# A hybrid attention and state-space layer: second group of weight blocks taken three pairs at a time instead of two

## The chip, the cores and the metric

One Trainium2 chip, of which the kernel uses one core. The metric is device time in microseconds, median of the runs.

## The reference

One layer of a streaming encoder on x of 1024 tokens by 2048 features, float32. One input projection gives everything; half of the width goes through sparse attention, half through a Mamba-2 scan; one output projection and a LayerNorm end it. Cut to what matters here:

```
u = jnp.einsum('bsd,de->bse', h, w_in[layer])            # 2048 x 6752
q, k, v, z_attn, q_idx, k_idx, w_idx, z_ssd, xbc, dt_raw = _split_cols(u, IN_WIDTHS)
o_attn = _dsa_attention(q, k, v, q_idx, k_idx, w_idx) * jax.nn.silu(z_attn)   # indexer, top 256 keys, softmax
o_ssd = _ssd_mixer(xbc, z_ssd, dt_raw, ...)              # conv, scan in chunks, gated norm
mixed = jnp.concatenate([o_attn, o_ssd], axis=-1)
sub = jnp.einsum('bse,ed->bsd', mixed, w_out[layer])
h = _layer_norm(DEEPNORM_ALPHA * h + sub, ln_g[layer], ln_b[layer])
```

## The kernel before, in words

**Products.** Weights and activations are split into a high and a low part (`wh`, `wl`; `xh`, `xl`), and a float32 product is three matmuls: high by high, high by low, low by high. A block of weights is 128 output columns by 1024 features, so one product of a block with 512 tokens is 8 x 3 = 24 matmuls of 512 columns into one PSUM bank. The high part is a copy on ACT, the low part a subtraction on DVE, seldom on POOL (`w_split`).

**Fewer products.** Two output tiles, two halves of the features and two halves of the tokens make a 2 x 2 x 2 problem that the kernel solves with seven products instead of eight (Strassen, in Winograd's form). So output tiles go in pairs. `PLAN` has two groups of pairs: the first (index 0) of eight, the second (index 1) of fourteen, numbered 0 to 13 here: 0 to 5 are the scan's x, B and C (`xbc`), 6 to 13 gates (`zs` with `z`).

**Stages.** A group runs in four stages (`ph` 0 to 3). In stages 0, 1 and 2 every pair has two products (`f` 0 and 1, here the pair's *first* and *second* product). They take two sets of x: stage 0 the two halves of x, stage 1 the sums M2 and M3, stage 2 the sums S1 and S4. In stage 3 a pair has one product. The second product of a pair goes on in the PSUM bank of its first: the first opens it, and its partial result has to be read out before the second goes on. In stage 0 ACT reads it (`t_save`, an ACTIVATE `u<-pj`, then a DMA to DRAM); in stage 1 DVE adds a saved sum to it (`t_u`), in stage 2 too (`t_comb`), both a TENSOR_TENSOR `u<-pj,u`. The second product waits for that (`p.after` in `emit_t`). Within a stage the pairs are taken in `couples`: the first products of all pairs of a couple, then their second ones.

**Weights.** A product of stage 0 loads one block; a first product of stage 1 loads three, of which two sums are made on DVE or POOL (`t_wacc`): one is for it, the other stays in its `wr` buffer for the pair's second product. In stage 2 a first product loads two and keeps one. There are six `wr` buffers for raw blocks, three `wh`, three `wl` (line 592). PSUM has four banks `pj` for the products, three `a` and one `o` for the rest; sums of attention and scan that find no `o` may take a `pj` while three or more are free (`avail`, `new`).

**The order of the work.** `Layer.run` walks the list of products that `units` made, 24 matmuls in four parts. Ahead of each part `Flow.pump` lets tasks run (generators that yield what they need next): copies, top-k, scan, attention, weight sums. A task may go ahead when the engine it needs is no further past PE by the kernel's own clock than a fixed slack (`SLACK` in `Flow.ready`, doubled for priority 0). So the instruction order of every engine is fixed when the program is built, with a model of times that also decides between DVE and POOL (`pick`), and a change in the list of products moves all later work. On the chip each engine runs its own list in order and waits on semaphores. While the second group starts, the top-k search over four blocks of keys runs on ACT, in counts (`u<-s,sm`, `u<-u,sm`: a Sign with a sum) whose thresholds DVE sets between them, and the scans of the first tokens start.

All instructions are issued through one helper, so each carries line 312; the names of the tiles tell them apart.

Of the kernel before, what the change touches and what calls it, by code (L numbers as in the profile page):

```python
# [582 lines left out]
class Layer:  # L583
# [20 lines left out]
    def units(self):  # L604

        pieces, work = [], []
        self.hooks = {}
        self.sets = []
        self.mate = {}

        def put(p, listed=True):
            if listed:
                work.append((len(pieces), None))
            pieces.append(p)
            return len(pieces) - 1

        def plain(h, tile, u, n):
            kind, j = tile
            t = ORDER.index(tile)
            p = Piece("T", h, t, u, load=(("w", t, u),), n=n + u, open=u == 0, close=u == 1, key=(h, t),  # L620
                      s0=256 if (kind == "qi" and h == 0) else 0)
            if u == 1:
                p.done = lambda ps: self.fl.add(getattr(self, "t_" + kind)(h, j, ps), 0, f"{kind}{j}h{h}", self.fl.t + 100)
            put(p)

        for pairs in PLAN:
            if isinstance(pairs, tuple):
                h, tiles, end = pairs
                n = len(self.sets)
                self.sets += [("x", h, 0), ("x", h, 1)]  # L630
                for part in [tiles[:3]] + [[t] for t in tiles[3:-end]] + [tiles[-end:]]:
                    for u in range(2):
                        for tile in part:
                            plain(h, tile, u, n)
                continue
            gi = GROUPS.index(pairs)
            if self.sets[-2:] != [("x", 0, 0), ("x", 0, 1)]:
                self.sets += [("x", 0, 0), ("x", 0, 1)]
            base = len(self.sets) - 2
            self.sets += [("f", "M2"), ("f", "M3"), ("f", "S1"), ("f", "S4"), ("x", 1, 1)]  # L640
            couples = [list(range(c, min(c + 2, len(pairs)))) for c in range(0, len(pairs), 2)]
            if len(couples[-1]) == 1:
                couples[-2:] = [couples[-2] + couples[-1]]
            for ph in range(4):
                if (gi, ph) in ((0, 2), (1, 0)):
                    self.hooks.setdefault(len(pieces), []).append(lambda on=gi == 0 and ph == 2: setattr(self.fl, "resting", on))
                for couple in [int(k) if k.isdigit() else k for k in OPENING] if (gi, ph) == (0, 0) else couples:
                    if isinstance(couple, str):
                        tile = ("misc", 0) if couple == "m" else QI["abcdefgh".index(couple)]
                        for u in range(2):  # L650
                            plain(0, tile, u, base)
                        continue
                    couple = couples[couple] if isinstance(couple, int) else couple
                    for f in range(1 + (ph < 3)):
                        for c in couple:
                            i = put(self.product(gi, c, pairs[c], ph, f, base + 2 * ph + f))
                            if f:
                                self.mate[gi, c, ph] = i
                            if ph and (ph, f) != (1, 1):
                                self.hooks.setdefault(max(i - 1, 0), []).append(lambda gi=gi, c=c, ph=ph, f=f: self.pre_ld(gi, c, ph, f))  # L660
        end = {}
        for i, p in enumerate(pieces):
            end[p.n] = i
        for i in end.values():
            pieces[i].last = True
        freed = sorted(end, key=end.get)
        for n in range(2, len(self.sets)):
            at = end[freed[n - 2]] - 2
            self.hooks.setdefault(at, []).append(lambda n=n: self.request(n))
        self.n_t = len(pieces)  # L670
        self.hooks.setdefault(self.n_t - 6, []).append(lambda: self.forms(0))
        self.hooks.setdefault(12, []).append(self.form_tasks)
        for half in range(2):
            self.hooks.setdefault(12, []).append(lambda half=half: self.fl.add(self.t_wsum(half), 5, "wsum"))
        for n in range(7):
            for d in range(2):
                for j in range(4):
                    if n < 6 or 4 * d + j < 8 - SKEW:
                        work.append((len(pieces), (0, 1, 2, 3)))
                    name = PRODUCTS[n][1]  # L680
                    pieces.append(Piece("O", n, d, j, load=(("o", name, d, j),)))
        for sts in ((0,), (1,), (2,), (3,)):
            work += [(len(pieces) - SKEW + j, sts) for j in range(SKEW)]
        return pieces, work
# [1672 lines left out]
```

## Time and profile before

| | us |
|---|---|
| median of 3 runs | 1664.8 (1663.27 to 1667.5) |
| profiled execution | 1667.98, its span 1666.1 |
| PE busy | 1620.1 (97% of the span) |
| DVE busy | 1321.7 (79%) |
| ACT busy | 1002.0 (60%) |
| POOL busy | 197.3 (12%) |
| mean granted TensorE clock | 0.992 |

The first group ends and the second begins at about 573 us; its stages 0, 1, 2 and 3 run to about 769, 1008, 1219 and 1313 us, and the output projection follows. A timeline row has start and length in us, engine, line, operation, out<-in, shape, count, and in brackets how long the engine stood idle before it and what ended that. Matmuls overlap in the pipeline, so their rate is read from start to start and not from their length. A row of the windows has the stretch, then the busy time of PE, PEld (weight loads), DVE, ACT and POOL with their instructions in brackets, the granted clock, the share of DMA and GB/s.

### The profile page before, as it was taken

How to read it: one execution, taken by the hardware profiler on the slowest of the kernel's cores; microseconds unless marked ns; L12 is line 12 of the kernel's file. 1: busy time of each engine (PE TensorE's matmuls, PEld its weight loads, DVE VectorE, ACT ScalarE, POOL GpSimd, SP SyncE). 2: the span in 40 equal slices, each digit the busy share in tenths (PEclk: the TensorE clock that was granted, in tenths of full speed). 3: DMA queues.
4: the chain of work that ended last, by engine and by line, in shares of the span. 5: the costliest groups of instructions: out<-in, count | busy, mean ns of one | idle time of the engine just before them, and what ended most of it. 6: DMA issues, size and time to landing. Idle time of an engine off the chain costs nothing. (4 is left out here: it accounts for less than half of the span.)

```text
span 1666.1 us, 23979 instructions
## 1 busy us (share of the span) xinstructions
PE 1620.1 (97%) x7996; PEld 1340.9 (80%) x7996; DVE 1321.7 (79%) x2429; ACT 1002.0 (60%) x1770; POOL 197.3 (12%) x215
## 2 busy tenths in 40 slices
PE   9999999999998989999999999999999999999997
PEld 7787777888787768888888888888877888888885
DVE  5889998997778866788676669875787687659998
ACT  4555666779787788776344456776866555532330
POOL 0100010000000000122212202222010000100110
PEclk9999999999999999999999999999999999999999
DMA  8177574789768856687786584656988889668664
GB/s 309 52 280 258 189 262 168 268 303 334 290 230 324 294 196 234 235 304 277 260 288 218 180 286 161 210 171 210 334 284 307 316 300 325 215 232 274 220 202 152
DMA packets 192387, 414.48 MB, mean 249 GB/s; under 512 B 19720, under 2 KB 55688, under 8 KB 192264
## 3 DMA queue, kind: packets, MB, share of 16 engines
q1 hardware_dynamic: 191832, 412.56, 71.7%
q8 instruction: 63, 1.03, 0.2%
q14 instruction: 60, 0.49, 0.1%
q10 hardware_dynamic: 432, 0.39, 0.1%
HBM read 308.94 MB, written 103.94 MB: 248 GB/s over the span
## 5 line engine op out<-in xcount | busy, mean ns | idle before, releaser
L312 PE MATMUL pj<-xh,wh 128*128 128x512 f32 (+1 forms) x1496 | 585.7, 392 | 14.5 <-ACT u L312 6.0
L312 PE MATMUL pj<-xh,wl 128*128 128x512 f32 (+1 forms) x1496 | 573.6, 383 | 5.1 <-DVE wl L312 5.1
L312 PE MATMUL pj<-xl,wh 128*128 128x512 f32 (+1 forms) x1496 | 573.0, 383 | 0.0
L312 DVE TENSOR_TENSOR wl<-wr,wh 128x1024 fp32r<-128x1024 f32 (+2 forms) x236 | 282.4, 1201 | 172.4 <-ACT wh L312 170.4
L312 PEld LDWEIGHTS pj<-xh,wh 128*128 128x128 f32 x1496 | 283.8, 190 | 68.6 <-issue 7.5
L312 PEld LDWEIGHTS pj<-xh,wl 128*128 128x128 f32 x1496 | 283.5, 190 | 63.1 <-DVE wl L312 7.3
L312 PEld LDWEIGHTS pj<-xl,wh 128*128 128x128 f32 x1496 | 284.0, 190 | 49.1
L312 ACT ACTIVATE wh<-wr 128x1024 fp32r<-128x1024 f32 (+2 forms) x242 | 248.1, 1031 | 120.0 <-PE pj L312 82.8
L312 PE MATMUL a<-u,u 128*128 128x512 f32 (+3 forms) x736 | 172.8, 354 | 7.6 <-DVE s L312 4.4
L312 PEld LDWEIGHTS a<-u,u 128*128 128x128 f32 x736 | 120.7, 189 | 42.5 <-DVE s L312 18.6
L312 ACT ACTIVATE u<-a 128x512 fp32r<-128x512 f32 (+4 forms) x115 | 53.2, 479 | 153.3 <-DVE u L312 58.0
L312 ACT ACTIVATE u<-s,sm 128x640 bf16<-128x640 int16 (+7 forms) x132 | 129.7, 983 | 22.1 <-DVE sm L312 20.0
L312 DVE TENSOR_TENSOR u<-u,u 128x512 f32<-128x512 f32 (+6 forms) x204 | 128.6, 645 | 5.7 <-DMA u<-wo 1.3
L312 PE MATMUL pj<-wh,xh 128*128 128x512 f32 x310 | 125.2, 404 | 0.5 <-DVE u L312 0.5
L312 PE MATMUL pj<-wh,xl 128*128 128x512 f32 x310 | 121.0, 390 | 0.0
L312 PE MATMUL pj<-wl,xh 128*128 128x512 f32 x310 | 121.0, 390 | 0.0
L312 ACT ACTIVATE a<-a 128x512 f32<-128x512 f32 (+3 forms) x160 | 77.1, 505 | 68.3 <-PE a L312 65.5
L312 ACT ACTIVATE u<-u 128x512 f32<-128x512 f32 (+4 forms) x146 | 80.1, 558 | 52.4 <-DVE u L312 43.9
L312 DVE TENSOR_TENSOR u<-pj,u 128x512 f32<-128x512 f32 (+2 forms) x112 | 74.7, 668 | 45.7 <-PE pj L312 42.2
L312 DVE TENSOR_TENSOR wr<-wr,wr 128x1024 f32<-128x1024 f32 (+1 forms) x81 | 99.8, 1233 | 0.8 <-DMA wr<-wt 0.4
L312 POOL TENSOR_SCALAR s<-s,sm 128x640 f32<-128x640 f32 (+7 forms) x64 | 63.8, 1011 | 124.0 <-DVE sm L312 97.4
L312 DVE SCALAR_TENSOR_TENSOR u<-cv,cw,u 128x512 f32<-128x512 f32 x96 | 73.0, 766 | 6.7 <-ACT u L312 3.5
(259 smaller groups left out, 2200.3 us busy)
## 6 DMA issues: line engine op xcount, KB each, us to landing
wr<-wt SPq DMA_DIRECT2D x187, 512.0 KB
u<-u SPq DMA_DIRECT2D x110, 256.0 KB
wr<-t SPq DMA_DIRECT2D x44, 512.0 KB
u<-wo SPq DMA_DIRECT2D x64, 256.0 KB
ts<-u SPq DMA_DIRECT2D x64, 256.0 KB
wr<-ts SPq DMA_DIRECT2D x32, 512.0 KB
s<-xt SPq DMA_DIRECT2D x24, 512.0 KB
t<-wr SPq DMA_DIRECT2D x22, 512.0 KB
```

Source lines behind the costliest of these rows:

```text
L312: f(*args, **kw)
```

## The change

In `units`, where the pairs of a group are cut into couples, the length goes from 2 to 2 + `gi`, the index of the group. The first group keeps its couples of two. The second has five runs in place of seven couples: pairs 0-2, 3-5, 6-8, 9-11 and 12-13. The rule for a last couple of one pair, below it, does not apply in either.

```
-            couples = [list(range(c, min(c + 2, len(pairs)))) for c in range(0, len(pairs), 2)]
+            couples = [list(range(c, min(c + 2 + gi, len(pairs)))) for c in range(0, len(pairs), 2 + gi)]
```

So in stages 0 to 2 the list reads: first products of pairs 0, 1, 2, second products of 0, 1, 2, first products of 3, 4, 5, and so on; before it was first 0, 1, second 0, 1, first 2, 3. Stage 3 is the same list as before. What the kernel's scheduler makes of it shows on every engine from there on. ACT in stage 0, before: the rows from the copy of pair 2's first product (`pj_1047`) to that of pair 3 (`pj_1053`); `s4_953` is a tile of the scan, `u_538` and `u_684` outputs of the top-k counts, `wh_...` high parts of weights.

```order
L312 ACTIVATE u_1049_6044<-pj_1047_6006 128x512
L312 ACTIVATE u_538_2976,sm_537_2975<-s4_109_745,sm_537_2975 128x896
L312 ACTIVATE u_538_2976,sm_537_2975<-s4_110_746,sm_537_2975 128x1024
L312 ACTIVATE wh_1051_6053<-wr_1009_5787 128x1024
L312 ACTIVATE u_684_3785,sm_683_3784<-u_440_2425,sm_683_3784 128x384
L312 ACTIVATE u_684_3785,sm_683_3784<-u_441_2426,sm_683_3784 128x512
L312 ACT_TABLE_LOAD
L312 ACTIVATE u_958_5501<-s4_953_5496 64x512 x2
L312 ACTIVATE s4_953_5496<-s4_953_5496,ac0_241 128x128 x8
L312 ACTIVATE u_1055_6107<-pj_1053_6057 128x512
L312 ACTIVATE wh_1056_6110<-wr_1024_5856 128x1024
```

And after, from the weights of pair 8's first product (`wh_1100`) to the copy of pair 6's (`pj_1103`):

```order
L312 ACTIVATE wh_1100_6413<-wr_1071_6180 128x1024
L312 ACT_TABLE_LOAD
L312 ACTIVATE u_958_5501<-s4_953_5496 64x512 x2
L312 ACTIVATE s4_953_5496<-s4_953_5496,ac0_241 128x128 x8
L312 ACT_TABLE_LOAD
L312 ACTIVATE u_1099_6401<-u_1099_6401 128x512
L312 ACTIVATE wh_1109_6474<-wr_1075_6213 128x1024
L312 ACTIVATE u_1112_6485<-pj_1103_6419 128x512
```

The scan's instructions on `s4_953` stood ahead of the copy of pair 3 and stand ahead of that of pair 6 now.

DVE in stage 1, before: up to the low part of the weights (`wl_1604`) for pair 8's first product; `pj_1582` is the bank of pair 7.

```order
L312 TENSOR_TENSOR sm_1583_8844<-sm_1583_8844 128x2
L312 TENSOR_SCALAR sm_1583_8844<-sm_1583_8844 128x2
L312 TENSOR_TENSOR u_1591_8896<-a_1589_8892,u_1590_8895 128x256
L312 TENSOR_TENSOR u_1599_8929<-pj_1582_8834,u_1552_8714 128x512
L312 TENSOR_TENSOR u_1595_8912<-a_1593_8906,u_1594_8911 128x512
L312 TENSOR_TENSOR u_1598_8922<-a_1596_8916,u_1597_8921 128x512
L312 RECIPROCAL sm_1583_8844<-sm_1583_8844 128x2
L312 TENSOR_TENSOR wl_1604_8945<-wr_1519_8541,wh_1603_8944 128x1024
```

And after, where `wl_1561` is that low part and `pj_1537` the bank of pair 7:

```order
L312 SCALAR_TENSOR_TENSOR u_1487_8398<-u_1487_8398,dn_222,o_1541_8691 128x256 x2
L312 TENSOR_TENSOR u_1518_8543<-u_1518_8543,u_1558_8780 128x512
L312 TENSOR_TENSOR u_1517_8541<-u_1517_8541,u_1518_8543 128x512
L312 TENSOR_TENSOR u_1559_8790<-pj_1537_8675,u_1535_8648 128x512
L312 TENSOR_TENSOR wl_1561_8795<-wr_1523_8581,wh_1560_8794 128x1024
L312 TENSOR_TENSOR wl_1563_8799<-wr_1468_8282,wh_1562_8798 128x1024
L312 TENSOR_TENSOR wl_1565_8803<-wr_1507_8454,wh_1564_8802 128x1024
```

In both the low part follows the sum that reads pair 7's first product; the products that stand between the two on PE are two before and none after.

## Prediction

> **What bounds the kernel now.** I read the page first, then the chain of waits for the tensor engine alone, cut to the second group (573 to 1313 us), then the timeline of PE and ACT where the longest waits end, then the windows for the clock.
>
> ```profile
> span 1666.1 us, 23979 instructions
> PE 1620.1 (97%) x7996; PEld 1340.9 (80%) x7996; DVE 1321.7 (79%) x2429; ACT 1002.0 (60%) x1770; POOL 197.3 (12%) x215
> ```
>
> PE is busy for 97% of the span, so at most 46 us of the span are idle PE, and an edit that adds and drops no work can win only from that idle and from matmuls that run slower than they could. In the second group, PE's waits, longest first (us in total, times, longest):
>
> ```profile
> PE pj L312 <- ACT u L312: 6.0, 2, 4.3
> PE a L312 <- DVE u L312: 2.1, 2, 1.5
> PE pj L312 <- ACT wh L312: 1.6, 1, 1.6
> ```
>
> The first row is 6.0 us in two waits alone; no row left out here is over 1.1. ACT's `u<-pj` is the copy of a pair's first product out of its PSUM bank (`t_save`, stage 0), and the waiting matmul is the first of the same pair's second product, which goes on in that bank. PE around the two:
>
> ```profile
> 583.38 0.39 PE L312 MATMUL pj<-xl,wh 128*128 128x512 f32 x1
> 583.60 0.39 PE L312 MATMUL pj<-xh,wl 128*128 128x512 f32 x1
> 585.73 0.50 PE L312 MATMUL pj<-xh,wh 128*128 128x512 f32 x1 [1.74 <-ACT u L312]
> ...
> 613.66 0.59 PE L312 MATMUL a<-u,u 128*128 128x256 f32 x2
> 618.56 0.80 PE L312 MATMUL pj<-xh,wh 128*128 128x512 f32 x1 [4.31 <-ACT u L312]
> 619.15 0.63 PE L312 MATMUL pj<-xl,wh 128*128 128x512 f32 x1
> ...
> 624.27 0.54 PE L312 MATMUL pj<-xl,wh 128*128 128x512 f32 x1
> 624.65 0.39 PE L312 MATMUL pj<-xh,wl 128*128 128x512 f32 x1
> 624.88 0.40 PE L312 MATMUL pj<-xh,wh 128*128 128x512 f32 x1
> ```
>
> In front of 585.73 the matmuls start 0.22 us apart (583.38, 583.60), so the next was due at 583.83: 1.90 us lost. The two 256-column matmuls at 613.66 were over in the queue by 613.90 (0.12 each, by half the 512-column step), and the next starts at 618.56: 4.66 us lost. It isn't over there: from 619.15 to 624.65 13 matmuls start in 5.50 us, 0.42 apart, where the full rate takes 2.95, and the one before took 0.59, so another 2.9 us go. The windows (span, busy PE, PEld, DVE, ACT, POOL, PEclk, DMA share, GB/s) say why:
>
> ```profile
> 573.00:590.00 17.00, 15.27 (x68) 12.32 (x67) 14.95 (x22) 14.72 (x28) 0.49 (x1) 1.00 0.66 232
> 605.00:620.00 15.00, 10.69 (x44) 8.33 (x43) 9.25 (x26) 14.69 (x29) 0.00 (x0) 0.92 0.52 181
> 617.70:624.50 6.80, 5.94 (x14) 4.74 (x15) 3.27 (x4) 6.75 (x13) 0.30 (x2) 0.50 0.59 195
> 650.00:665.00 15.00, 15.00 (x68) 12.43 (x67) 11.31 (x26) 13.39 (x22) 2.22 (x2) 1.00 0.80 270
> 665.00:680.00 15.00, 15.00 (x68) 12.43 (x67) 13.35 (x19) 9.75 (x19) 0.00 (x0) 1.00 0.91 299
> ```
>
> The granted clock is 0.50 in the 6.8 us from 617.7, and 1.00 in the window with the short wait. The Trainium skill, page "TensorE: Matmul & The Clock Gate", section "What's actually happening", has the clock halved after an idle window of about 3.4 us. By that rule a wait of 4.66 us costs its length and a spell at half clock, one of 1.90 only its length; the trace agrees with both.
>
> The other windows show ACT: 14.69 of 15 us, then 13.39, then 9.75. So up to about 665 ACT is nearly as full as PE; what it does ahead of the second copy:
>
> ```profile
> 595.25 0.62 ACT L312 ACTIVATE u<-u 128x512 f32<-128x512 f32 x1
> 595.78 0.59 ACT L312 ACTIVATE cv<-pj 128x512 f32<-128x512 f32 x1
> 596.40 0.81 ACT L312 ACTIVATE u<-cv,cw 128x512 f32<-128x512 f32 x1
> 597.12 1.03 ACT L312 ACTIVATE u<-s,sm 128x896 bf16<-128x896 f32 x1
> ...
> 607.45 0.58 ACT L312 ACTIVATE u<-pj 128x512 f32<-128x512 f32 x1
> 608.16 1.05 ACT L312 ACTIVATE u<-s,sm 128x896 bf16<-128x896 f32 x1
> ...
> 609.33 1.15 ACT L312 ACTIVATE u<-s,sm 128x1024 bf16<-128x1024 f32 x1
> ...
> 610.48 1.04 ACT L312 ACTIVATE wh<-wr 128x1024 fp32r<-128x1024 f32 x1
> 611.42 0.60 ACT L312 ACTIVATE u<-u,sm 128x384 bf16<-128x384 f32 x1
> ...
> 612.15 0.72 ACT L312 ACTIVATE u<-u,sm 128x512 bf16<-128x512 f32 x1
> ...
> 612.98 1.28 ACT L312 ACT_TABLE_LOAD   x1
> 614.28 1.28 ACT L312 ACTIVATE u<-s 64x512 f32<-64x512 f32 x2
> 615.58 2.44 ACT L312 ACTIVATE s<-s,ac 128x128 f32<-128x128 f32 x8
> 617.93 0.57 ACT L312 ACTIVATE u<-pj 128x512 f32<-128x512 f32 x1
> 618.41 1.04 ACT L312 ACTIVATE wh<-wr 128x1024 fp32r<-128x1024 f32 x1
> ```
>
> The row at 617.93 is pair 3's copy. Since pair 2's at 607.45 ACT has been through four top-k counts, a split, a table load and the scan's activations without a pause.
>
> **The change part by part.** Nothing is added or dropped: 98 products of 24 matmuls in the second group. A pair's second product follows its first after two others instead of one: a matmul step is 0.22 to 0.23 us (583.38 to 583.60, 624.65 to 624.88), 0.227 taken, and a product 24 x 0.227 = 5.45 us, so the copy has 10.9 us, not 5.45. Stages 0, 1 and 2 change; stage 3 has one product a pair. At the end of each stage the last five pairs become a run of three and a run of two, so the order in which x sets are released is that of before.
>
> *The first wait (585.73).* The matmul that waited is now the first product of pair 2, which opens a free bank. Its low half is there at 584.45 (the row below, 583.23 and 1.22), and its third matmul, the first to need it, is due at 584.29: 0.2 us of the 1.9 stay, and the product starts at 584.0 in effect. Gain 1.7.
>
> ```profile
> 583.23 1.22 DVE L312 TENSOR_TENSOR wl<-wr,wh 128x1024 fp32r<-128x1024 f32 x1
> ```
>
> *The second wait (618.56).* By the ACT rows shown with the change, the scan's block (`s4_953`) has moved from ahead of pair 3's copy to ahead of pair 6's, with another table load behind it. Pair 3's second product waits for nothing of it: gain 4.66 + 2.9 = 7.6. What may be late next is pair 6's copy. I walk ACT to it by start-to-start steps of the rows quoted: u<-u 0.53, cv<-pj 0.62, u<-cv 0.72, u<-pj 0.5, top-k counts 1.17 and 1.15 (896 and 1024 columns), 0.73 and 0.83 (384 and 512), split 0.95, table load 1.30, u<-s x2 1.30, s<-s x8 2.35. Both programs are equal on ACT up to the row at 595.25, so the new one goes on at 595.8. Up to the split for pair 3's first product the new order has eleven instructions: 0.5 + 1.17 + 1.15 + 0.95 + 0.73 + 0.83 + 0.62 + 0.72 + 1.17 + 1.15 + 0.95 = 9.9, so 605.7. From there to the end of pair 6's copy: 9 splits (8.6), 6 + 6 large counts (13.9), 5 + 5 small (7.8), 5 conv copies and 5 conv starts (6.7), 10 of the kind u<-u (5.3), 4 copies u<-pj (2.0), 2 table loads, u<-s and s<-s (6.3): 50.6, so 656.3. PE, from 584.0, has 13 products ahead of pair 6's second: 13 x 5.45 = 70.9, plus 4200 columns of scan work that the order puts between them (1.9 us at 0.227 per 512), so 656.8. ACT and PE arrive within 1 us of each other, if ACT never idles. Bounds: nothing, if ACT keeps this pace; 3 us, if it loses what the windows show it without work (0.3 of 15 us at 605 to 620, 1.6 at 650 to 665) once or twice more on the way. I take 1.0, nearer to the full windows.
>
> *Splits just in time.* At 605.7 the high half for pair 3's first product is ready, and PE comes to it at 584.0 + 4 x 5.45 = 605.8; DVE's low half needs about 1.2 us more (row below), 606.9 or later, and the third matmul is due at 606.3. Cost 0.6, between 0 and 2.
>
> ```profile
> L312 DVE TENSOR_TENSOR wl<-wr,wh 128x1024 fp32r<-128x1024 f32 (+2 forms) x236 | 282.4, 1201 | 172.4 <-ACT wh L312 170.4
> L312 DVE TENSOR_TENSOR u<-pj,u 128x512 f32<-128x512 f32 (+2 forms) x112 | 74.7, 668 | 45.7 <-PE pj L312 42.2
> ```
>
> In stage 1 the same happens to pair 8, third of its run: by the DVE rows shown with the change its low half stands behind the sum that reads pair 7's first product, and pair 8 is now PE's next product, not the third from there. So 0.67 + 1.20 = 1.9 us pass after pair 7's product, and the third matmul is due after 0.45: cost 1.5 (0 if attention matmuls fill it, 3 if the split on ACT is late too). No other product of the group has its low half behind the sum of the product just ended.
>
> *Buffers.* Three of the four PSUM banks `pj` are held through a run, not two; attention and scan sums that used spare `pj` banks move to the one bank `o`. Over the group they take the same columns, and by the order the background work stays within 8 us of its old place and is level at stage 3: 0, bounds -2 and 2.
>
> *Table loads.* The load at 612.98 lasts 1.28, and the next activation starts 1.30 after it. The Trainium skill, page "ScalarE: Activation LUTs", section "What ACT_TABLE_LOAD costs", adds a drain of about 1.38 us to each switch. By it pair 6's copy would come 2.8 us later and the sum below would be -3.4; the step of 1.30 us here shows no such drain.
>
> *Sum.* -1.7 - 7.6 + 1.0 + 0.6 + 1.5 = -6.2 us. The profiled execution took 1667.98 us around its span of 1666.1, 0.2% above the median of three, 1664.8; the waits are differences and carry over: 1664.8 - 6.2 = 1658.6. About 0.3%, 5.0 us, can be told from no change, so this is just on the far side of it. PE's other waits in the group are dealt anew, since every later instruction moves: I allow 5 us either way, two thirds of what one wait like the second costs with its spell at half clock.
>
> **The rivals.**
>
> *ACT is the bound of that stretch (no change).* Without its waits PE comes to pair 6 some 9 us earlier, and ACT has the same work to do. If it idles anywhere on the way, PE waits for it at pairs 3 to 8 instead. For: 14.69 of 15 us. Against: the walk, which meets PE within 1 us. Price 5 to 8 us given back: 1663 to 1666.
>
> *Third weights come late (slower).* Six buffers `wr` hold raw weights. In stage 1 a first product takes three loads and keeps one buffer until its second product, so in a run of three the third pair's loads go out only when both before it are summed:
>
> ```profile
> 870.03 1.65 SPq L312 DMA_DIRECT2D wr<-wt  x3
> 882.09 2.98 DVE L312 TENSOR_TENSOR wr<-wr,wr 128x1024 f32<-128x1024 f32 x2
> ```
>
> From first issue to the end of the second sum 15.0 us pass here; the split's two halves make it 17.
>
> ```profile
> 770.00:1008.00 238.00, 234.78 (x1290) 200.59 (x1289) 168.87 (x316) 111.86 (x207) 53.22 (x37) 1.00 0.74 251
> ```
>
> 28 products in 238 us are 8.5 us each. In the new order pair 8's last load stands two products ahead of its use, 17 us; before it was six. So it has no slack. It decides where loads land 4 us later than here: then PE idles over 3.4 us, the clock halves, and each such place costs 4 to 6 + 2.9. Pairs 2, 5, 8 and 11 are third; two of them cost some 16 us: 1675. Against: the other three have leads of three to four products, 26 us or more, and attention work can fill PE there.
>
> That the change does nothing is excluded by the order above.
>
> **How the numbers follow.** Forecast (waits go, little comes back) 0.62: 1658.6, give or take the 5 us dealt anew; a bit over two in three of it lies more than 5.0 us below 1664.8. ACT as the bound 0.22, nearly all within 0.3%. Late weights 0.16, nearly all slower. Faster 0.45, same 0.39, slower 0.16. The range reaches from 1651 (the sum with the lower bounds, -9.3, and 4 us of luck) to 1669 (ACT's rival and 3 us the other way); late weights lie outside.
>
> **What would show it.** Right: no PE wait on ACT `u` over 1 us at 580 to 660, PEclk 1.00 there, pair 6's second product starting within 1 us of its copy, a short wait on a `wl` at pair 8. Wrong: PE waits on ACT `u` or `wh` around 640 to 665 that add to 5 us or more (ACT as the bound); a wait on `wr` or `wl` over 3 us and a window at 0.50 in stage 1 (late weights); or equal waits there and the loss elsewhere, in which case the dealing anew outweighs the cause.

## The result, and the profile after

| | before | after |
|---|---|---|
| median, us | 1664.03 (1662.09 to 1667.5, 4 runs) | 1680.1 (1679.58 to 1681.32, 4 runs) |
| ratio, 95% interval | | 1.0093 (1.0076 to 1.0109) |
| profiled execution, us | 1667.98, span 1666.1 | 1681.32, span 1679.0 |

Slower by 15 to 16 us, where 6.2 us less were forecast. The page of the kernel after:

```profile
span 1679.0 us, 24003 instructions
PE 1624.5 (97%) x7996; PEld 1341.7 (80%) x7996; DVE 1322.3 (79%) x2419; ACT 1003.0 (60%) x1770; POOL 208.8 (12%) x225
```

The matmuls are the same 7996, and the share of busy PE is the same, so the time lies in waits and in matmuls at half clock. The waits of PE in the second group (573 to 1313 us, columns as before):

```profile
PE a L312 <- ACT u L312: 3.3, 1, 3.3
PE a L312 <- DVE u L312: 3.3, 4, 1.8
PE pj L312 <- ACT wh L312: 2.4, 1, 2.4
PE pj L312 <- DVE u L312: 1.8, 1, 1.8
PE pj L312 <- DVE wl L312: 1.8, 3, 1.1
```

The 6.0 us of `pj` on ACT `u` are gone. In their place stands a list of waits of another kind, the first of them a matmul into `a`, the background's bank. From 1313 to 1500 us, in the output projection, the kernel before had one row:

```profile
PE a L312 <- DVE u L312: 0.2, 1, 0.2
```

and the kernel after has these:

```profile
PE pj L312 <- ACT xh L312: 2.9, 1, 2.9
PE a L312 <- DVE xl L312: 0.8, 2, 0.5
PE a L312 <- DVE u L312: 0.8, 1, 0.8
PE pj L312 <- DVE xl L312: 0.7, 1, 0.7
```

These are waits on the splits of the output projection's x, in a part of the program whose list of products was not touched. The timeline of PE at the places that the prediction spoke of, and at the longest new waits:

```profile
584.65 0.50 PE L312 MATMUL pj<-xh,wl 128*128 128x512 f32 x1 [0.22 <-DVE wl L312]
...
619.07 0.50 PE L312 MATMUL pj<-xh,wl 128*128 128x512 f32 x1 [0.47 <-DVE wl L312]
...
656.18 0.40 PE L312 MATMUL pj<-xh,wl 128*128 128x512 f32 x1
659.90 2.15 PE L312 MATMUL a<-u,u 128*128 128x512 f32 x6 [3.32 <-ACT u L312]
...
878.79 0.39 PE L312 MATMUL pj<-xh,wl 128*128 128x512 f32 x1
881.55 0.50 PE L312 MATMUL pj<-xh,wh 128*128 128x512 f32 x1 [2.37 <-ACT wh L312]
881.88 0.40 PE L312 MATMUL pj<-xl,wh 128*128 128x512 f32 x1
883.35 0.79 PE L312 MATMUL pj<-xh,wl 128*128 128x512 f32 x1 [1.06 <-DVE wl L312]
...
1455.24 0.40 PE L312 MATMUL pj<-wh,xl 128*128 128x512 f32 x1
1458.53 0.50 PE L312 MATMUL pj<-wh,xh 128*128 128x512 f32 x1 [2.89 <-ACT xh L312]
```

At 584.65 and 619.07, about where the two old waits were, 0.2 and 0.5 us are left. By the steps (the matmul before, 0.23, then the wait) 3.5 us are lost at 659.90, 2.5 and 1.2 at pair 8 (881.55 and 883.35), 3.1 at 1458.53. Windows of the kernel after, columns as before:

```profile
573.00:590.00 17.00, 16.78 (x74) 13.56 (x73) 14.95 (x22) 14.57 (x27) 0.49 (x1) 1.00 0.65 223
605.00:620.00 15.00, 14.38 (x62) 11.14 (x61) 11.56 (x26) 14.50 (x27) 0.66 (x3) 1.00 0.61 206
650.00:665.00 15.00, 11.67 (x45) 8.94 (x44) 9.49 (x21) 13.62 (x28) 0.74 (x1) 0.89 0.86 281
660.40:663.80 3.40, 3.39 (x11) 2.59 (x10) 2.80 (x8) 2.15 (x5) 0.27 (x1) 0.50 0.84 302
882.30:889.10 6.80, 5.75 (x18) 4.78 (x19) 5.20 (x7) 2.29 (x4) 0.32 (x1) 0.50 0.60 176
1459.10:1462.50 3.40, 3.40 (x11) 2.76 (x11) 2.85 (x7) 2.79 (x7) 0.00 (x0) 0.50 0.03 7
```

605 to 620 went from 10.69 busy us to 14.38, and 650 to 665 from 15.00 to 11.67: the hole has moved by 45 us, half clock included. Each of the three long waits is followed by a spell at 0.50.

Where the whole loss stands can be added up. For each stage I take the time from its first matmul to that of the next, less the steps of the matmuls between (for each shape the lower quartile of its start-to-start steps); what is left is PE's *lost time*, waits and half clock together, in us. The 512-column step comes out as 0.226 or 0.227 us, so a column is good to about 1 us:

| profiled execution | stage 0 | stage 1 | stage 2 | stage 3 | output, products 1 to 3 | sum |
|---|---|---|---|---|---|---|
| before | 14.2 | 10.1 | 10.4 | 9.2 | 12.0 | 55.9 |
| after | 11.4 | 18.7 | 13.1 | 3.7 | 22.4 | 69.3 |

Outside these columns the two differ by under 1 us. The changed stages lost 8.5 us net, stage 3 won 5.5, and the first three products of the output projection lost 10.4. At the start of the output projection the two kernels were level (1313.1 and 1313.4 us); the background (attention and scan) had 2.7 us more of matmuls left there in the kernel after, by the same steps.

### The profile page after: what moved, and what is told of

Read it like the earlier page. It is cut to its first block, busy times and chain, and to the rows that moved or that the text cites. A ratio compares the mean times of both kernels' runs of the same rounds, so it can differ in the third digit from the quotient of the medians.

```text
span 1679.0 us, 24003 instructions
## 1 busy us (share of the span) xinstructions
PE 1624.5 (97%) x7996; PEld 1341.7 (80%) x7996; DVE 1322.3 (79%) x2419; ACT 1003.0 (60%) x1770; POOL 208.8 (12%) x225
## 4 chain that ended last, share of the span: by engine, by line
PE 37%; DVE 6%; ACT 3%; issue 3%; DMA 1%; POOL 0%; DVEq 0%; SPq 0%; ACTq 0%
PE pj L312 27%; PE a L312 7%; DVE u L312 3%; PE o L312 3%; ACT s L312 1%; DVE xl L312 1%; ACT wh L312 1%; DVE xh L312 1%; DVE wl L312 1%; ACT u L312 1%; DVE wr L312 1%; ACT xh L312 0%; DMA s<-arow 0%; DVE s L312 0%; DMA u<-wo 0%
## 5 line engine op out<-in xcount | busy, mean ns | idle before, releaser
L312 PE MATMUL pj<-xh,wh 128*128 128x512 f32 (+1 forms) x1496 | 585.0, 391 | 10.1 <-DVE u L312 6.2
L312 PEld LDWEIGHTS pj<-xh,wl 128*128 128x128 f32 x1496 | 283.8, 190 | 67.4 <-DVE wl L312 11.8
L312 DVE TENSOR_TENSOR u<-u,u 128x512 f32<-128x512 f32 (+6 forms) x204 | 136.4, 680 | 10.8 <-ACT u L312 5.7
L312 PE MATMUL pj<-wh,xh 128*128 128x512 f32 x318 | 129.5, 407 | 4.0 <-ACT xh L312 2.9
L312 PE MATMUL pj<-wh,xl 128*128 128x512 f32 x318 | 124.9, 393 | 0.0
L312 PE MATMUL pj<-wl,xh 128*128 128x512 f32 x318 | 124.4, 391 | 0.0
L312 POOL TENSOR_SCALAR s<-s,sm 128x640 f32<-128x640 f32 (+7 forms) x64 | 67.8, 1074 | 189.1 <-DVE sm L312 154.2
L312 DVE SCALAR_TENSOR_TENSOR s<-a,wsc,s 128x512 f32<-128x512 f32 (+3 forms) x120 | 73.1, 644 | 3.6 <-ACT a L312 1.3
```

The costliest lines, as they stand in the source:

```text
L312: f(*args, **kw)
```

## The experiments

All kernels were compared with the kernel before on the same chip, whose median there was 1664.1 to 1665.1 us. The first question was which stage costs. Theory A: each stage has its own cost by the mechanism seen in it. Theory B: every change of the list deals the waits anew. Theory C: the banks.

**Runs of three in one stage alone** (`t0`, `t1`, `t2` for stages 0, 1, 2; here stage 1).

```
+            threes = [list(range(c, min(c + 3, len(pairs)))) for c in range(0, len(pairs), 3)]
...
-                for couple in [int(k) if k.isdigit() else k for k in OPENING] if (gi, ph) == (0, 0) else couples:
+                for couple in [int(k) if k.isdigit() else k for k in OPENING] if (gi, ph) == (0, 0) else threes if gi and ph in (1,) else couples:
```

> Runs of three in stage 0 alone; stages 1 and 2 in couples as before. Theory A (each stage has its own cost, set by the mechanism seen there, and the tail is late because the scan fell behind in stages 1 and 2): the two waits on the copies go, the new wait near pair 6 stays; stage 0 is 3 to 7 us shorter and little comes back, so 1658 to 1663. Theory B (any change of the list deals all later waits anew, the stage does not matter): anything from 1657 to 1681, with the gain of stage 0 lost after 770 us.

Measured 1665.47, ratio 1.0000 (0.9991 to 1.0009): the upper end of theory A was 1663.

> Runs of three in stage 1 alone. Theory A: the weights of the third pair come late there (pair 8: waits on its split and its low half with a spell at half clock), so stage 1 loses 7 to 10 us as in the changed kernel, and the scan falls behind, so the output projection starts with waits on xh and xl worth some 5 us more: 1671 to 1680. Theory B: no wait above 2 us on a split at pair 8, time anywhere from 1657 to 1681.

Measured 1678.16, ratio 1.0078 (1.0063 to 1.0093). The time is A's, the place is not: stage 1 itself lost 0.6 us less than before.

> Runs of three in stage 2 alone. Theory A: the changed kernel lost 2.6 us in stage 2 and won 5.4 in stage 3, where the old half clock at 1280 us went; alone it should be within 4 us of the kernel before, 1661 to 1669. Theory B: anywhere from 1657 to 1681.

Measured 1677.9, ratio 1.0075 (1.0060 to 1.0090): A is wrong. Lost time by stage, as above:

| profiled execution | stage 0 | stage 1 | stage 2 | stage 3 | output, 1 to 3 | sum |
|---|---|---|---|---|---|---|
| stage 0 alone | 11.8 | 7.3 | 8.0 | 8.5 | 17.5 | 53.1 |
| stage 1 alone | 13.8 | 9.5 | 16.8 | 8.1 | 19.8 | 68.0 |
| stage 2 alone | 14.4 | 10.1 | 12.8 | 8.4 | 21.7 | 67.4 |

In none of the three does most of the loss lie in the stage that was changed. It comes in a later stage, and in all three in the output projection. They don't add up either: 0, 13 and 13 alone, 15 together. Stage 0 alone came to the output projection 12.8 us ahead of before, with 6.6 us more of background still to do, and was level by its fourth product.

**Fewer banks for the background.** Couples as before, but no sum of attention or scan may take a `pj` in stages 0 to 2.

```
-            return self.avail("o") + max(self.avail("pj") - 2, 0)
+            return self.avail("o") + max(self.avail("pj") - 2 - 2 * self.tight, 0)
```

> The kernel before, couples of two, but sums of attention and scan may take no pj bank in stages 0 to 2 of the second group, which is what runs of three leave them. Theory C (the banks are the cause: with one bank o the scan and the attention go slower, their last results are late, and the output projection waits for its splits): 8 to 15 us slower than before, 1672 to 1680, with the waits on xh and xl between 1340 and 1470 us as in the changed kernel. Theory A without the banks: within 3 us of 1664.

Measured 1695.92, ratio 1.0182 (1.0165 to 1.0199), over twice what theory C expected. It came to the output projection at 1291.9 us, 21 us ahead of before, but with 11 us more of background left, and lost 45.0 us in the first three products there (12.0 before). Two of PE's waits from 573 to 1500 us, the first for a sum in the one bank `o`, the second of the kind that C named:

```profile
PE o L312 <- DVE s L312: 4.4, 5, 2.4
PE pj L312 <- DVE xl L312: 3.2, 1, 3.2
```

**The scan's end cut off.** Since the loss ends in the output projection, and its third product needs the scan's rows of the first tokens, theory D made the scan's end its bound. Four kernels leave those rows out: the third product takes attention's rows (`A21`) a second time in place of the scan's (`A22`), so it does not wait for the scan's end, and the result is not the layer's.

```
-        parts = dict(S1=("A21", "A22", "A11"), S3=("A11", "A21"), S4=("A12",)).get(name, (name,))
+        parts = dict(S1=("A21", "A21", "A11"), S3=("A11", "A21"), S4=("A12",)).get(name, (name,))
```

> Couples of two, and the third product of the output projection takes its x without the scan's rows of the first tokens (attention rows in their place), so the scan's end is needed only at the fifth product, some 90 us later. Theory D (the scan's end is what the start of the output projection is bound by): the kernel before had little waiting there, so 0 to 3 us faster than before: 1661 to 1665. It is the base for the three that follow. Rival (it isn't the scan but the attention, or DVE's load in general): the same number.

Measured 1664.88, ratio 1.0006 (0.9995 to 1.0016).

> The same cut with runs of three in stage 0 alone. That kernel stood 12.8 us ahead of the one before at the start of the output projection, 8.4 of it less waiting, and had it all back by the fourth product. Theory D: with the scan's end out of the way 5 to 9 us of it stay, 1654 to 1660. Rival: the waits on xh and xl come anyway, within 2 us of the cut with couples.

Measured 1664.32, ratio 0.9999 (0.9988 to 1.0011).

> The same cut in the changed kernel, which lost 3.0 us of waiting in the second group and 10.4 in the output projection. Theory D: the 10.4 go, 3 to 5 us slower than the cut with couples: 1665 to 1669. Rival: it stays 11 to 15 us slower than that, 1674 to 1680.

Measured 1677.29, ratio 1.0077 (1.0059 to 1.0094), 12.4 us over the cut with couples.

> The same cut with runs of three in stage 2 alone, which was level with the kernel before at the start of the output projection and 10.5 us behind at its fourth product, with the scan's last block 18 us late. Theory D: level, within 3 us of the cut with couples. Rival: 9 to 13 us slower than that.

Measured 1672.11, ratio 1.0042 (1.0024 to 1.0061), 7.2 over the cut with couples, 5.8 under stage 2 alone without the cut. So D fell as the account of the whole: nothing came back with stage 0, and 2.8 us in the kernel after. With stage 2 alone about half did (5.8 of 13 us), less than D expected and more than its rival, so there the scan's end is part of the cost. What the splits wait for shows on ACT in the kernel after, ahead of the wait at 1458.53:

```profile
1456.79 0.28 ACT L312 ACTIVATE u<-a 128x128 f32<-128x128 f32 x1 [2.08 <-DVE u L312]
1457.33 0.63 ACT L312 ACTIVATE xl<-xh 128x512 f32<-128x512 f32 x1 [0.26 <-DVE xh L312]
1457.86 1.66 ACT L312 ACTIVATE xh<-u 128x512 fp32r<-128x512 f32 x3
```

The three splits `xh<-u` stand behind two background steps (`u<-a`, `xl<-xh`) that wait for DVE. DVE made its last `u` of 128x512 ahead of them by 1452.1, and POOL none after that, so by these rows it is their place in ACT's list, and not their data, that makes them late. The cut leaves the list nearly as it was.

**More banks for the background, and another slack.** The sums may take a `pj` while two are free, in the kernel before, the kernel after and stage 0 alone (`- 1` in place of `- 2` in the line above); and the scheduler's slack, with nothing else changed (`SLACK = 3000.0` in place of `2650.0`).

> Couples of two, but sums of attention and scan may take a pj bank while two are free, not three. The list of products is that of before; 19 thousand columns of background are left at the start of the output projection, not 21. Theory C (banks for the sums set the pace of the background, and what is left of it at the output projection stands among its splits): faster by 2 to 6 us, 1658 to 1662, with less waiting from 1313 us on. Rival (the products need the banks; taking one makes first products wait for it): level or slower, 1664 to 1670.

Measured 1691.56, ratio 1.0152 (1.0133 to 1.0172).

> The changed kernel with the same rule for the sums, so that with three banks held the fourth can be lent. 18 thousand columns are left at the start of the output projection, not 23. Theory C: the 10 us lost in the output projection go, the 3 us of waiting in the second group stay or become a few less: 1664 to 1670, so 10 to 16 us faster than the changed kernel. Rival (late weights and splits in stage 1 are the cause): 1675 to 1682, level with it.

Measured 1686.6, ratio 1.0129 (1.0114 to 1.0144).

> Runs of three in stage 0 alone with the same rule. 16 thousand columns left at the start of the output projection, not 27 as without the rule. Theory C: the gain of stage 0 (8 us less waiting up to the output projection) isn't given back: 1654 to 1660. Rival: 1662 to 1668.

Measured 1690.86, ratio 1.0154 (1.0139 to 1.0168).

> Couples and banks as before; the scheduler's slack is 3000 instead of 2650, which happens to leave 26 thousand columns of background at the start of the output projection (21 before). Nothing of the products or banks differs. Theory C in its wider form (what is left of the background there decides, whatever left it): slower by 5 to 15 us, 1670 to 1680, with the waits on xh and xl after 1313 us. Rival (only the runs of three and their banks cost): within 3 us of 1664.

Measured 1682.18, ratio 1.0109 (1.0090 to 1.0129). Lost time in four of these kernels, as above (the second group starts within 3 us of its place before):

| profiled execution | stage 0 | stage 1 | stage 2 | stage 3 | output, 1 to 3 | sum |
|---|---|---|---|---|---|---|
| couples, fewer banks | 12.9 | 8.1 | 4.7 | 8.3 | 45.0 | 79.0 |
| couples, more banks | 13.4 | 19.2 | 13.6 | 11.3 | 19.0 | 76.5 |
| kernel after, more banks | 11.2 | 16.3 | 25.5 | 13.1 | 9.6 | 75.7 |
| couples, slack 3000 | 17.7 | 12.6 | 12.9 | 12.7 | 20.5 | 76.4 |

As a forecast of the time C is refuted: with more banks and less background left all three are slower than the kernel before, by 27, 22 and 26 us. Its first half came true in the kernel after: the output projection lost 9.6 us instead of 22.4, but stages 2 and 3 lost 21.8 more. Besides, fewer banks, more banks and another slack, all with couples, are all slower by 17 to 31 us, though their products are those of the kernel before. What they share is that the steps of the background stand elsewhere among the products. That made theory E: the placing of the background decides, each list gets one, and that of the kernel before is a good one. F and G are its rivals, F that the output projection is bound by the background's end, G that runs of three cost by themselves.

**The background held in place.** A record of the kernel before says at which quarter of a product each step of the background was let go; in place of the slack rule a step now goes when its quarter has come and its inputs and buffers are there.

```
     def pump(self, room=2000.0):
+        if FROM <= self.at < UPTO:
+            return self.place(room)
...
+                    if task and (self.ready(task) or self.at >= at + OVERDUE and self.fits(task)):
```

> Runs of three in stage 0 alone, but every step of attention, scan, top-k and weight sums is let go at the quarter of a product at which the kernel before has it (a list in the kernel in place of the slack rule; with couples this gives the kernel before, instruction for instruction). From the end of stage 1 on the background stands where it stood. Theory E (the new placing of the background gives the gain back): the 7 us of the two waits stay, 1656 to 1661. Theory F (the gain can't be kept: the output projection is bound by when the background ends): 1663 to 1667, with waits on xh and xl after 1313 us.

Measured 1664.42, ratio 0.9999 (0.9987 to 1.0010): E is wrong for stage 0. With the background back at its places by the end of stage 1 (from stage 2 on PE's rows are those of before, one for one), the gain is at most 2.2 us, and the output projection lost 12.0 us as before, so F isn't it either. Stage 0 lost 10.1 us in that profile; new waits stand there, the longest for the scan's sums (the helper is line 323 in the held kernels):

```profile
636.73 0.44 PE L323 MATMUL o<-s,u 128*64 128x128 f32 x4 [2.14 <-DVE s L323]
```

Why so little was to be had there is told in the next section.

> Runs of three in stage 2 alone with the background held at its places of before from stage 3 on (within stage 2 it falls behind by up to 10 thousand columns, since the banks are held). Theory E: the 13 us that stage 2 cost with free placing go, 1662 to 1668. Theory G (runs of three cost by themselves, through their banks): 1672 to 1680 as with free placing.

Measured 1693.2, ratio 1.0178 (1.0158 to 1.0197), 15 us slower than with free placing. Stage 2 itself lost 27.3 us (10.4 before). PE's waits there (1005 to 1232 us):

```profile
PE pj L323 <- DVE u L323: 5.1, 2, 4.9
PE o L323 <- DVE u L323: 3.0, 4, 1.0
```

> Runs of three in stages 0 and 2 with the background held at its places of before. Theory E: about the sum of the two above, 1655 to 1662. Theory F or G: 1665 or more.

Measured 1693.02, ratio 1.0171 (1.0154 to 1.0187): stage 0 adds nothing. So with three banks held the old placing isn't to be had in stage 2 without waits for the sums that free banks (`u<-pj`) and for `o`; the scheduler, left free, avoids most of them by another placing. The loss in the output projection did not come back: with stage 2 held its first three products lost 22.1 us, with free placing 21.7. The order there was not quite the old one either: with stage 2 held the scan's eight `s<-s,ac` stand on ACT behind a copy `xh<-xl`, and in the kernel before ahead of it. So these two runs do not decide between E and G for stage 2.

**Runs of three and couples on other placings.**

> The changed kernel with the scheduler's slack at 3000; couples at that slack took 1682.2. Theory E (each list is one draw; couples at 2650 were a good one): runs of three are not slower than couples here, 1667 to 1685. Theory G: 8 to 16 us slower than couples at the same slack, 1690 to 1698.

Measured 1672.54, ratio 1.0037 (1.0018 to 1.0055): 9.6 us *faster* than couples at that slack. The longest row of PE's waits from 573 to 1500 us there, with couples:

```profile
PE pj L312 <- ACT u L312: 8.2, 4, 4.8
```

and with runs of three:

```profile
PE pj L312 <- ACT wh L312: 3.6, 2, 2.1
```

> Couples of two at a slack of 3500, where 15 thousand columns of background are left at the start of the output projection (21 in the kernel before). Theory C, less background left is better: 1655 to 1662. Theory E, each placing is one draw of waits: anywhere from 1664 to 1690, as the other placings were 1672 to 1696.

Measured 1684.16, ratio 1.0113 (1.0082 to 1.0145).

> Runs of three at a slack of 3500, with 24 thousand columns left. Theory G, runs of three cost by themselves: 10 to 16 us slower than couples at that slack. Theory E: 1664 to 1690, the difference to couples of either sign; theory C: 8 us or more slower than couples there, since 9 thousand columns more are left.

Measured 1684.11, ratio 1.0117 (1.0088 to 1.0146), the same as couples. The three pairs:

| slack | couples | runs of three | difference |
|---|---|---|---|
| 2650 | 1664.0 | 1680.1 | +16.1 |
| 3000 | 1682.2 | 1672.5 | -9.6 |
| 3500 | 1684.2 | 1684.1 | 0.0 |

The slack holds for the first group too. At 3500 the second group starts at 579.4 us with couples and at 580.0 with runs of three, 573.0 before, so about 7 of the 19 us stand ahead of it.

G is wrong as a cost of its own that is always there: the sign follows the placing. C is wrong once more (15 thousand columns left by the count in the expectation, and 19 us slower). E is what the runs leave; a kernel with runs of three in stage 1 or 2 and the whole old placing, which would show it directly, is not among them. No version tried beats the kernel before; stage 0 alone, free or held, ties with it.

## Why the prediction was wrong, step by step

Two steps failed: the worth of a wait, read from one profile, and the 5 us allowed for the waits that are dealt anew. The steps follow in the prediction's order.

*The first wait* was right: a copy needs no wait, and 0.22 us on `wl` stay, as said.

*The second wait, gain 7.6*: gone, as said, but 7.6 was what it cost in that one execution. Other profiles here ran the same instructions up to there. PE's row at the two waits in stage 1 alone:

```profile
585.69 0.79 PE L312 MATMUL pj<-xh,wh 128*128 128x512 f32 x1 [2.60 <-ACT u L312]
618.52 0.50 PE L312 MATMUL pj<-xh,wh 128*128 128x512 f32 x1 [2.86 <-ACT u L312]
```

and in the kernel before with the cut, the second one:

```profile
618.80 0.50 PE L312 MATMUL pj<-xh,wh 128*128 128x512 f32 x1 [2.81 <-ACT u L312]
```

2.8 us, not 4.31. From the first wait's end to the second's it is 32.83 us in the kernel before and in stage 1 alone (618.56 - 585.73, 618.52 - 585.69), and 32.82 or 32.83 in all eight profiles that run these instructions; the second wait and the half clock behind it cost 3.4 to 7.7 us in them. The windows between them in the kernel before:

```profile
585.00:618.00 33.00, 28.52 (x126) 23.20 (x126) 22.97 (x51) 26.35 (x51) 1.19 (x4) 1.00 0.59 201
```

and in stage 1 alone:

```profile
585.00:618.00 33.00, 29.96 (x126) 24.46 (x126) 22.91 (x51) 26.35 (x51) 1.19 (x4) 0.95 0.59 200
```

ACT is busy for 26.35 us in both, with the same 51 instructions; PE had some half clock in one and took 1.4 us longer, and the wait shrank by as much. So ACT paces this stretch, and PE's wait is what is over. "The waits are differences and carry over" failed: the profiled execution, 1667.98 us, stood 3 to 4 us above the median, and the long wait with its spell was part of that. Over six profiles with couples there stage 0 lost 11.8 to 14.4 us; over four with runs of three placed freely, 11.4 to 13.1. The prediction's four terms for stage 0 add up to 7.7 us less; the means differ by 1.

*ACT's walk to pair 6's copy, 1.0 (0 to 3)*, met the copy and missed what PE would wait for. ACT in the kernel after:

```profile
653.72 1.28 ACT L312 ACT_TABLE_LOAD   x1
655.02 0.63 ACT L312 ACTIVATE u<-u 128x512 f32<-128x512 f32 x1
655.55 1.04 ACT L312 ACTIVATE wh<-wr 128x1024 fp32r<-128x1024 f32 x1
656.50 0.58 ACT L312 ACTIVATE u<-pj 128x512 f32<-128x512 f32 x1
656.98 1.03 ACT L312 ACTIVATE u<-s,sm 128x896 bf16<-128x896 f32 x1
...
659.45 0.40 ACT L312 ACTIVATE u<-u 128x256 fp32r<-128x256 f32 x1
```

Pair 6's copy starts at 656.50 and the next instruction at 656.98 (walked: 656.3). But PE was not at pair 6 yet. At 656.18 it had done 18 of the 24 matmuls of pair 8's first product, and between these and pair 6's second product stood nine background matmuls of 512 columns; by the steps pair 6 was due at 659.8 (walked: 656.8, with less background in between), so the copy itself made nothing late. What PE waited for was the first of the nine, `a<-u,u`, due at 656.41. ACT makes its operand at 659.45, behind the copy and three counts: 3.5 us and a spell at half clock. Another table load stands in this walk, and the next activation starts 1.30 after it (653.72 to 655.02). By the Trainium skill, page "ScalarE: Activation LUTs", section "What ACT_TABLE_LOAD costs", a drain of about 1.38 us comes with each switch. An estimate from that puts the copy 2.8 us later, and the measured step shows no such drain here. So the first rival, ACT as the bound, was right for stage 0: "PE waits for it at pairs 3 to 8 instead".

*Splits just in time, 0.6 (0 to 2)*: by the steps 0.3 us at pair 3's first product, the one that the term was about (its third matmul starts at 607.32), and 0.6 at pair 5's (619.07), together within the bounds.

*Pair 8 in stage 1, 1.5 (0 to 3)*: 2.5 + 1.2 us and a spell at half clock, over the upper bound; that bound was for a split that is late on ACT, and that is what came. It has the look of the second rival, late weights, but not its cause. DVE in the kernel after, the last weight sum ahead of it:

```profile
867.94 1.75 DVE L312 TENSOR_TENSOR wr<-wr,wr 128x1024 f32<-128x1024 f32 x1
```

and ACT:

```profile
878.82 0.83 ACT L312 ACTIVATE s<-s,sm 128x640 f32<-128x640 f32 x1 [2.44 <-DVE sm L312]
...
879.65 0.81 ACT L312 ACTIVATE s<-s,sm 128x640 f32<-128x640 f32 x1
...
880.46 2.94 ACT L312 ACTIVATE wh<-wr 128x1024 fp32r<-128x1024 f32 x3
```

The weights were summed by 869.7, eleven us earlier; POOL summed none there. Three splits at a time stood on ACT behind the exponentials of attention, which waited for DVE. And in stage 1 alone, with pair 8 third of its run too, no such loss is in stage 1.

*Buffers, 0 (-2 to 2)*: wrong in stage 2, where the old placing with three banks held cost 16.9 us of lost time.

*"PE's other waits in the group are dealt anew: I allow 5 us either way"* is the step on which the forecast broke. It was a term of the size of the wait removed, and measured it is 13 to 16 for three of the four lists tried, and 17 to 31 where the list was left alone and only banks or slack, and with them the placing, changed. It also stopped at the group's end, while the larger part (10.4 of 13.4 us in the kernel after) came behind it. The step that said how far the background is moved ("within 8 us of its old place and level at stage 3") was no measure of its cost: 1.7 us more of background at the start of the output projection (stage 2 alone) went with 9.7 us more lost there.

The time, 1680.1, is near the second rival's 1675, by another way. What stays open is why the kernel before's placing is better than the others, and so what in the placing costs the 16 us: its own rows show few waits where the others have many, and no single quantity tried (banks, columns left, the scan's end) orders the kernels. Runs of three at a placing searched for them weren't tried.

## What to carry to other kernels

Where a scheduler places background work at build time, a change of the main list is two changes; before a gain of a few us is forecast, the spread of placings has to be measured by a change that leaves the list alone (here another slack: 17 and 19 us, of the latter about 7 in the first group). A wait for an engine that is nearly full in that stretch isn't a gain to be had: compare two profiles of the same instructions, and if the distance between the ends of two waits is fixed (32.83 us) while their length varies, the other engine sets the pace. And the account has to go past the changed stages to the next place where background and products must meet.

## What the runs showed of the hardware

The half clock keeps to a grid. In the kernel after spells begin at 660.4, 882.3, 1220.2 and 1459.1 us; the distances 221.9, 337.9 and 238.9 are 65, 99 and 70 times 3.413, and these spells are 3.4 or 6.8 long. In each of the 20 profiles the spells start whole multiples of 3.4133 us apart. By the Trainium skill, page "TensorE: Matmul & The Clock Gate", section "What's actually happening", the clock goes by windows of about 3.4 us that run on by themselves. The trace agrees. A wait's price therefore hangs on where it falls in these windows. The wait of 2.81 us in the kernel before with the cut, which straddles two of them, was followed by no spell,

```profile
617.50:624.50 7.00, 5.70 (x25) 4.74 (x26) 3.03 (x4) 6.97 (x13) 0.30 (x2) 1.00 0.54 159
```

while the one of 2.83 in stage 2 alone, at the same instruction, ran into one:

```profile
617.50:624.50 7.00, 7.00 (x18) 5.50 (x19) 4.29 (x6) 6.68 (x12) 0.30 (x2) 0.57 0.68 201
```

The prediction read from one profile that a wait of 1.90 us (by the steps) costs its length alone. In stage 2 alone the same matmul starts 2.06 us late by the steps, and half clock comes with the next window (starts 0.42 us apart):

```profile
584.64 0.50 PE L312 MATMUL pj<-xh,wh 128*128 128x512 f32 x1 [1.90 <-ACT u L312]
...
586.27 0.63 PE L312 MATMUL pj<-xh,wh 128*128 128x512 f32 x1
586.69 0.63 PE L312 MATMUL pj<-xl,wh 128*128 128x512 f32 x1
```

I divided all 20 profiles from 560 to 1500 us into the windows of their own grid and added up, in each window at full clock, what PE lost by late starts. All 44 windows that lost more than 2.26 us were followed by half clock, and none of the 5281 that lost less than 1.46; of those between, 18 were and 60 were not. So in these runs about 2 us of idle PE within one window bring half clock, and a wait need not last 3.4 us.
